# Making the two column halves of attention's P v product neighbours on TensorE in a hybrid attention and mLSTM layer

## The chip, the cores and the metric

The kernel runs on one core of a Trainium2 chip. The metric is the device time in microseconds (us) of one execution. The engines are named as the profile names them: PE is the matmul side of TensorE and PEld its weight loads, DVE is VectorE, ACT is ScalarE, POOL is GpSimd and SP is SyncE, which here only issues DMAs.

## The reference

One layer mixes sliding window attention with an mLSTM (a gated linear recurrence), adds a residual and a layer norm, and runs a SwiGLU feed-forward block with a second layer norm. The model width is 1024. There are 2048 prompt tokens behind 16 meta tokens, and 64 sample tokens. Attention has 8 query heads of 64 features, and two key and value heads, so four query heads share each of them. Cut to what matters here:

```python
s = einsum('nbqkgd,nbskd->nbkgqs', q, k) * HEAD_DIM ** -0.5      # kd = 64, k: the 2 kv heads, g: 4 query heads of each
s = where(mask, s + alibi, -inf)                                 # window of 128
p = exp(s - mx);  p = p / (sum(p) + exp(sink - mx))
att = einsum('nbkgqs,nbskd->nbqkgd', p, v)                       # the P v product
y  = concat([head_norm(att), head_norm(sigmoid(o) * h_m)])       # h_m: the mLSTM
x1 = layer_norm(alpha * x + y @ w_out)
out = layer_norm(alpha * x1 + (silu(x1 @ w_gate) * (x1 @ w_up)) @ w_down)
```

## The kernel before

The work has three phases. Phase 1a and 1b project the input onto q, k, v, the gates and the conv channels; phase 2, over five groups of 384 to 440 tokens, does the output projection, the layer norms and the feed-forward block. All large products are written as three matmuls of split operands, in the helper `mm3` (L123, L124 and L125: upper bits by upper bits, upper by lower, lower by upper). They are the bulk of PE's work. Their weights are fetched by SP (`wtile`, L995), rounded to the upper bits on ACT (L111), and the rest is taken on DVE or POOL (L120).

Attention and the mLSTM are background work. For each of the 16 chunks of 128 prompt tokens there is one generator `bg_attn(c)` and one `bg_ml(c)`; `both` steps them side by side, and `pace` takes steps of the queue between the large products, from the second column group of phase 1b on. `bg_drain` finishes the chunks that the next token group needs. The program written in this order goes through the framework's scheduler, which sets each engine's final order: by operands, buffers and its own estimate of when each operand is ready, an instruction may be moved past others of its engine. On the chip each engine then takes its queue in that order, and a semaphore wait at the head holds what stands behind it.

Within a chunk `bg_attn` works as follows. The scores of the 8 heads go to the SBUF tile `Pt`. For each half `j` of the 256 keys, the four heads of kv head `g` are transposed on PE into a PSUM tile (L542, matmuls with the identity in `C`), and ACT copies that tile to the SBUF tile `p` (L544, one copy for each `g`). Then, for each `g`, one matmul (L548) multiplies the 64 value columns of kv head `g` with `p`:

```python
        for c0, n, j in halves:
            ps = []
            for g in range(2):
                pt = bps()
                for t in range(4):
                    PE.transpose(pt[0:n, 128 * t:128 * t + 128], Pt[:, 4 * g + t, c0:c0 + n], ident)   # L542
                p = t2k("pt", [128, 512], 4)
                A.copy(p[0:n], pt[0:n])                                                                # L544
                ps.append(p)
            yield
            for g in range(2):
                PE.matmul(o[64 * g:64 * g + 64, :], lhsT=vt[0:n, j, 64 * g:64 * g + 64], rhs=ps[g][0:n],   # L548
                          start=(j == 0), stop=(j == 1), skip_group_check=True)
            yield
```

The weights of that matmul are 128 rows by 64 columns, and the result of `g` lies on the PSUM partitions 64 g to 64 g + 63: the two matmuls use different column halves of the array. They are float32, and each appears in the trace as two passes of 512 columns. In all there are 16 chunks, 2 halves of the keys and 2 kv heads: 64 matmuls, 32 pairs. After the second pair ACT reads `o` (L553), and a norm of each head follows (`att_rstd`, L470 to L478).

The other background matmuls that stand beside them are those of the mLSTM (L667, L677 and L678) and the transposes of its output (L592).

Of the kernel before, what the change touches and what calls it, by code (L numbers as in the profile page):

```python
# [20 lines left out]
NS = 64  # L21
# [10 lines left out]

# column offsets of the packed constants and parameters
C_T, C_U, C_BD, C_ID, C_QS, C_US, C_MS, C_SEL, C_SS = 0, 256, 384, 512, 640, 644, 708, 772, 780
# [15 lines left out]
def tile_hymba(  # L50
# [16 lines left out]
    cp = ctx.enter_context(tc.tile_pool(name="const", bufs=1))  # L67
    # the first weights and columns of phase 1b lie where the background work is later
    early = ExitStack()
# [10 lines left out]

# [1 line left out]
    C = cp.tile([128, C_END], F32, name="C")  # L82
# [16 lines left out]

    # token-major gate results: columns (chunk, head), chunk 0 the meta tokens  # L100
    NC4 = (NCH + 1) * 4
# [5 lines left out]

# [1 line left out]
    def hi_of(eng, out, src):  # L109
# [7 lines left out]
    def split(eng, hi, lo, src, veng=V):  # L117
        """src (float32) -> hi, its upper bits, and lo, the rest."""
        hi_of(eng, hi, src)
        return veng.tensor_tensor(out=lo, in0=src, in1=hi.bitcast(F32), op=ALU.subtract)  # L120
# [6 lines left out]
    def rsqrt(v, y, t):  # L127
        """y = v ** -0.5 (v positive, float32): integer seed and Newton's steps."""
        V.tensor_scalar(out=t.bitcast(I32), in0=v.bitcast(I32), scalar1=1, scalar2=None,
                        op0=ALU.logical_shift_right)  # L130
        V.tensor_scalar(out=y.bitcast(I32), in0=t.bitcast(I32), scalar1=-1.0,
                        scalar2=float(0x5F3759DF), op0=ALU.mult, op1=ALU.add)
        for _ in range(3):
            V.tensor_tensor(out=t, in0=v, in1=y, op=ALU.mult)
            V.scalar_tensor_tensor(out=t, in0=t, scalar=-0.5, in1=y, op0=ALU.mult, op1=ALU.mult)
            V.scalar_tensor_tensor(out=y, in0=t, scalar=1.5, in1=y, op0=ALU.add, op1=ALU.mult)

    flip = [0]

    # weights and columns of phase 1b; the order of its tiles: c first, the conv and the maps follow  # L140
    MT = [5, 6, 7, 8, 0, 1, 2, 3, 4]
    NEARLY = 4
    # the last columns' q and k come later, while the first layer norm runs
    NMT = [9, 9, 9, 9, 9 - NLATE]
# [35 lines left out]

# [1 line left out]
    with ExitStack() as s1:  # L182
# [39 lines left out]

        # the first two tiles of tokens go through the weights as they arrive
        x0, x1 = (load_x(tiles[i], ((0, 2), (2, KD)), "v") for i in range(2))
# [4 lines left out]
        for k in range(KD):  # L229
# [8 lines left out]
            for i in range(2):  # L238
                mm_a(start[i], i, k)
        # nothing else is fetched before the weights of this phase  # L240
        with tc.issue_after(w1dma[0].ins):
            constants()
        for i in range(NCH + 1):
# [23 lines left out]
            vm = st[:, 128:128 + 516].rearrange("p (h e) -> p h e", e=129)  # L267
            # v, centred over the head dimension for the attention
            sm = tp.tile([128, 2], F32, tag="sm", name="sm", bufs=2)
# [31 lines left out]

# [1 line left out]
    def gates():  # L303
# [24 lines left out]
        V.tensor_scalar(out=u, in0=e, scalar1=1.0, scalar2=None, op0=ALU.add)  # L328
        # log1p(e) = ln(u) + (e - (u - 1)) / u, u = fl(1 + e)
        V.scalar_tensor_tensor(out=d, in0=u, scalar=-1.0, in1=e, op0=ALU.add, op1=ALU.subtract)  # L330
# [6 lines left out]
        Us = C[0:NS, C_US:C_US + NS]  # L337
        # b: running sums of log f, token-major and as rows (chunk, head)
        b = bps()
# [35 lines left out]
        V.tensor_copy(bl, rb[0:1, 0:NC4])  # L375
        # m of each chunk's end: m = b_last + max(m, max a)
        for h in range(4):
# [14 lines left out]
        A.dma_start(out=GW.rearrange("r g t -> r (g t)"), in_=gw)  # L392
        # back to tokens on partitions
        mb = bps()
# [7 lines left out]
        V.tensor_tensor(out=ENM[:, 0:NC4], in0=gt[:, 0:NC4], in1=bsb[:, 0:NC4], op=ALU.add)  # L402
        # the running sequences: segments of 8 tokens
        cms = tmp(NS, 4)
# [34 lines left out]

# [1 line left out]
    def t2k(tag, shape, bufs, dt=F32):  # L441
        return bp.tile(shape, dt, tag=tag, name=tag, bufs=bufs)

    def spread_rstd(sq, n, nc_, ind, ni, space):
        """sq: tiles [128 features, nc_ * n tokens] to be added; sums over the features with ind [128, ni] give the
        variances with tokens on partitions; then their rsqrt, spread over the features (PSUM)"""
        vp = space()
# [19 lines left out]
    def att_rstd(o, w):  # L467
        """rsqrt of the variances of the heads of o ([128 (kv, d), w], centred), over all of d"""
        sq = t2k("pt", [128, 512], 4)
# [14 lines left out]
    def bg_attn(c):  # L484
# [52 lines left out]
# [3 lines that stand above are left out]
# [3 lines left out]
                p = t2k("pt", [128, 512], 4)  # L543
                A.copy(p[0:n], pt[0:n])  # L544
                ps.append(p)
            yield
            for g in range(2):
                PE.matmul(o[64 * g:64 * g + 64, :], lhsT=vt[0:n, j, 64 * g:64 * g + 64], rhs=ps[g][0:n],  # L548
                          start=(j == 0), stop=(j == 1), skip_group_check=True)
            yield  # L550
# [12 lines left out]
    def mlstm_tail(nd, n, enm, o, y0):  # L563
        """nd: two PSUM tiles [n, 2, 129] of num | den; writes the normed output to y columns y0."""
        dn = t2k("dn", [128, 64], 2)
# [264 lines left out]
    def both(*gens):  # L830
        """steps of all of them, side by side"""
        gens = list(gens)
        while gens:
            for x in list(gens):
                if next(x, 0) == 0:
                    gens.remove(x)
            yield

    # background queue: (column up to which it counts, columns needed, number of steps, generator)
    queue = [(NM, NM, 1, bg_meta())]  # L840
# [19 lines left out]
    def bg_drain(col):  # L860
        """finish everything that columns up to col need"""
        while done[0] < len(queue) and queue[done[0]][0] <= col:
# [16 lines left out]
    def out_q(pool, p, m, c0, w):  # L879
        """feature tile m of q (m < 4) or k of the columns from c0 on"""  # L880
        ev = pool.tile([128, 426], F32, tag="ev", name="ev", bufs=4) if pool is not None else x_tile(F32)
# [9 lines left out]
    def need(g):  # L891
        # chunks are whole: the column where the last one that group g reads ends
        e = ends[g]
# [3 lines left out]

# [1 line left out]
    with ExitStack() as s1:  # L899
# [5 lines left out]
        for g, w in enumerate(IN_GROUPS):  # L905
            c0 = sum(IN_GROUPS[:g])
            wp_ = w if g < 4 else w - NS      # meta and prompt columns of the group

            def conv(h):
                """conv + SiLU of head h over the group's columns -> 2 * c_act"""  # L910
                e, es = ext[g, h]
# [76 lines left out]

# [1 line left out]
    with ExitStack() as s2:  # L990
# [11 lines left out]
        def weights():  # L1002
            """the tiles of the weights in the order of their use"""
            for g in range(len(FF_GROUPS) + 1):
# [71 lines left out]
        def norm(z, w, s, space, fast=False):  # L1076
            """z: tiles, s: the sum of all of them, or of all but the last if fast;
            centres z in place, returns 1 / standard deviation (PSUM)"""
            mu = space()
# [24 lines left out]
        def ln1(z, w, s, out, fast=False, marks={}):  # L1104
            ry = yield from norm(z, w, s, gps, fast)
            for k in range(KD):
# [5 lines left out]
                if k % 2 == 0:  # L1112
                    continue
                # the rest of the even tile on DVE, of the odd one on Pool
                ze, be = z[k - 1][:, 0:w], Q[:, Q_L1B + k - 1:Q_L1B + k]
# [42 lines left out]
        def down(z, h, s, w, zs, adds):  # L1158
            """adds the products of slice s of the hidden features to z"""
            n = SLICES[s]  # L1160
# [25 lines left out]
        x1 = []  # L1186
        # the chain to the first x1 goes ahead of the background work
        mark = {7: None}
# [56 lines left out]

# [1 line left out]
def _consts():  # L1247
# [30 lines left out]
def _layout(x):  # L1278
    """the arrays of setup_inputs() as the kernel reads them"""
    f = {n: np.asarray(a) for n, a in x.items()}  # L1280
    cat = np.concatenate
    X = cat([f["meta_tokens"], f["x_prompt"][0], f["x_sample"].reshape(NS, D)], 0)

    def feat(w):          # (K, N) -> [p, k, N]
        return w.reshape(-1, 128, w.shape[1]).transpose(1, 0, 2)

    def mtile(w):         # (K, M) -> [p, m, k * 128 + j]
        k, m = w.shape
# [76 lines left out]
```

## Time and profile before

| | |
|---|---|
| time, median of 3 runs | 2522.82 us (2521.44 to 2523.54) |
| span of the profiled execution | 2522.3 us |
| PE busy | 2465.8 us (98%) |
| PEld busy | 2267.9 us (90%) |
| DVE busy | 1506.0 us (60%) |
| ACT busy | 954.8 us (38%) |
| POOL busy | 330.5 us (13%) |
| matmul passes on PE | 13135 |
| mean granted TensorE clock | 0.991 |

The profile gives no time for the profiled execution other than its span; the span lies 0.5 us under the median of the runs. PE's busy time counts a matmul from its start to its modelled end, and neighbours overlap. So what a matmul costs is read from the start of one to the start of the next, in the timeline.

### The profile page before, as it was taken

Reading aid. Unit: us, or ns where it says so; the run is one execution under the profiler, and the core shown is the slowest. Engines: PE = TensorE matmul, PEld = TensorE weight load, DVE = VectorE, ACT = ScalarE, POOL = GpSimd, SP = SyncE. Lnnn points to the kernel's source line nnn. Section 1 sums busy time; section 2 is a strip of 40 time slices with the busy share of each in tenths; the row PEclk is TensorE's granted clock in tenths of the full one; section 3 lists DMA queues with packets and bytes.
Section 4 is the critical chain, followed back from the end, with each engine's and each line's share of the span. In section 5 each row is a group of like instructions: output and inputs, shape, how many; then the busy total and the mean of one; then the engine's idle time right before and its main releaser. Section 6 shows DMA issues by size and latency. Waiting matters only on the chain.

```text
span 2522.3 us, 34923 instructions
## 1 busy us (share of the span) xinstructions
PE 2465.8 (98%) x13135; PEld 2267.9 (90%) x13135; DVE 1506.0 (60%) x3129; ACT 954.8 (38%) x1730; POOL 330.5 (13%) x253
## 2 busy tenths in 40 slices
PE   9999999998999999999999999999999999999997
PEld 8999888887999888888989889889999999999997
DVE  6223466547876887656664976666676434664444
ACT  3112444345434444424333543443353223442332
POOL 1000000021000015210011500100330000520001
PEclk9999999999999999999999999999999999999998
DMA  7223533664444543554443354444344333343442
GB/s 234 88 89 89 168 113 123 124 218 118 137 133 136 150 142 94 179 155 142 122 137 115 103 186 123 129 126 123 100 147 134 115 109 113 113 137 115 119 126 77
DMA packets 197330, 327.89 MB, mean 130 GB/s; under 512 B 31010, under 2 KB 133498, under 8 KB 197146
## 3 DMA queue, kind: packets, MB, share of 16 engines
q1 hardware_dynamic: 170400, 294.29, 39.9%
q10 hardware_dynamic: 26762, 31.36, 3.8%
q8 instruction: 104, 1.70, 0.3%
q14 instruction: 64, 0.52, 0.1%
HBM read 281.59 MB, written 44.99 MB: 129 GB/s over the span
## 4 chain that ended last, share of the span: by engine, by line
PE 88%; DVE 4%; DMA 4%; ACT 1%; issue 1%; POOL 0%; SPq 0%; ACTq 0%; DVEq 0%; POOLq 0%
PE gps L123 24%; PE gps L125 24%; PE gps L124 24%; PE bps L548 2%; PE bps L123 2%; PE bps L125 2%; PE bps L124 2%; PE bps L513 2%; DMA w<-in_wo 1%; PE bps L542 1%; PE gps L932 1%; DVE w L120 1%; PE bps L677 1%; PE bps L650 1%; PE bps L667 1%
## 5 line engine op out<-in xcount | busy, mean ns | idle before, releaser
L125 PE MATMUL gps<-x,w 128*128 128x440 f32 (+4 forms) x2240 | 797.3, 356 | 3.9 <-POOL w L120 3.3
L123 PE MATMUL gps<-x,w 128*128 128x440 f32 (+4 forms) x2240 | 790.4, 358 | 7.9 <-DVE z L1070 4.5
L124 PE MATMUL gps<-x,w 128*128 128x440 f32 (+4 forms) x2240 | 795.6, 356 | 0.6 <-DVE x L1117 0.5
L111 ACT CAST w<-w 128x1024 fp32r<-128x1024 f32 (+2 forms) x423 | 400.4, 947 | 783.9 <-DMA w<-in_wd 277.5
L120 DVE TENSOR_TENSOR w<-w 128x1024 fp32r<-128x1024 f32 (+2 forms) x391 | 442.8, 1133 | 361.9 <-ACT w L111 197.9
L123 PEld LDWEIGHTS gps<-x,w 128*128 128x128 f32 x2240 | 421.8, 188 | 32.3 <-DVE z L1070 6.2
L125 PEld LDWEIGHTS gps<-x,w 128*128 128x128 f32 x2240 | 421.6, 188 | 24.6 <-POOL w L120 5.0
L124 PEld LDWEIGHTS gps<-x,w 128*128 128x128 f32 x2240 | 421.2, 188 | 23.8 <-issue 5.2
L123 PE MATMUL gps<-hh,w 128*128 128x440 f32 (+2 forms) x880 | 314.4, 361 | 0.0
L125 PE MATMUL gps<-hh,w 128*128 128x440 f32 (+2 forms) x880 | 312.5, 356 | 0.0
L124 PE MATMUL gps<-hl,w 128*128 128x440 f32 (+2 forms) x880 | 312.0, 356 | 0.0
L120 POOL TENSOR_TENSOR w<-w 128x1024 fp32r<-128x1024 f32 x32 | 77.0, 2407 | 778.0 <-ACT w L111 676.8
L123 PEld LDWEIGHTS gps<-hh,w 128*128 128x128 f32 x880 | 165.6, 188 | 9.9 <-issue 3.5
L125 PEld LDWEIGHTS gps<-hh,w 128*128 128x128 f32 x880 | 165.6, 188 | 8.7 <-issue 1.0
L124 PEld LDWEIGHTS gps<-hl,w 128*128 128x128 f32 x880 | 165.8, 188 | 7.9 <-issue 1.5
L1167 DVE SCALAR_TENSOR_TENSOR z<-z,gps 128x440 f32<-128x440 f32 (+2 forms) x160 | 92.9, 589 | 68.6 <-PE gps L125 67.9
L111 ACT CAST hh<-hr 128x440 fp32r<-128x440 f32 (+2 forms) x110 | 59.9, 545 | 157.2 <-DVE hr L1153 157.0
L1153 DVE SCALAR_TENSOR_TENSOR hr<-ft,gps 128x440 f32<-128x440 f32 (+2 forms) x110 | 64.9, 590 | 83.7 <-PE gps L125 83.3
L120 DVE TENSOR_TENSOR hl<-hr,hh 128x440 fp32r<-128x440 f32 (+2 forms) x110 | 82.3, 748 | 29.1 <-ACT hh L111 28.7
L1150 ACT ACTIVATE ft<-gps 128x440 f32<-128x440 f32 (+2 forms) x110 | 57.3, 521 | 104.1 <-PE gps L125 103.5
L1061 POOL TENSOR_TENSOR zs<-zs,z 128x440 f32<-128x440 f32 (+2 forms) x58 | 81.7, 1408 | 101.7 <-DVE z L1070 66.6
L120 DVE TENSOR_TENSOR x<-x 128x426 fp32r<-128x426 f32 (+4 forms) x80 | 48.0, 612 | 78.3 <-ACT x L111 56.6
(338 smaller groups left out, 3150.0 us busy)
## 6 DMA issues: line engine op xcount, KB each, us to landing
w<-in_wg SPq DMA_DIRECT2D x110, 512.0 KB, 3.7
w<-in_wu SPq DMA_DIRECT2D x110, 512.0 KB, 3.7
w<-in_wd SPq DMA_DIRECT2D x80, 384.0 KB, 3.2
w<-in_wd SPq DMA_DIRECT2D x80, 320.0 KB, 3.0
w<-in_wo SPq DMA_DIRECT2D x40, 512.0 KB, 3.9
FM<-ev ACTq DMA_DIRECT2D x52, 213.0 KB, 2.0
TM<-st ACTq DMA_DIRECT2D x16, 578.0 KB, 3.9
vmo<-TM SPq DMA_DIRECT2D x16, 514.0 KB, 3.5
```

The costliest lines, as they stand in the source:

```text
L111: A.copy(out, src)
L120: return veng.tensor_tensor(out=lo, in0=src, in1=hi.bitcast(F32), op=ALU.subtract)
L123: PE.matmul(out, lhsT=wh, rhs=xh, start=start, stop=False)
L124: PE.matmul(out, lhsT=wh, rhs=xl, start=False, stop=False)
L125: PE.matmul(out, lhsT=wl, rhs=xh, start=False, stop=stop)
L513: PE.matmul(s[g][:, j, 0:nk], lhsT=x[r, 2 * tt + j, :], rhs=y[r, 0:nk], start=(i == 0), stop=(i == 2))
L542: PE.transpose(pt[0:n, 128 * t:128 * t + 128], Pt[:, 4 * g + t, c0:c0 + n], ident)
L548: PE.matmul(o[64 * g:64 * g + 64, :], lhsT=vt[0:n, j, 64 * g:64 * g + 64], rhs=ps[g][0:n], start=(j == 0), stop=(j == 1), skip_group_check ...
L1061: G.tensor_tensor(out=s[:, 0:w], in0=s[:, 0:w], in1=z[m][:, 0:w], op=ALU.add)
L1150: A.activation(out=t[:, 0:w], in_=pgt[:, 0:w], func=AF.Tanh, scale=0.5)
L1153: V.scalar_tensor_tensor(out=hr[:, 0:w], in0=t[:, 0:w], scalar=0.5, in1=pu[:, 0:w], op0=ALU.mult, op1=ALU.mult)
L1167: V.scalar_tensor_tensor(out=zm, in0=zm, scalar=ALPHA if s == 0 else 1.0, in1=p[:, 0:w], op0=ALU.mult, op1=ALU.add)
```

## The change

When `g` is 0, the matmul gets one more dependency: on the copy of `g` = 1, whose result it doesn't read. Nothing is computed otherwise, and no instruction of an engine is added or removed. The other differences of the two files are comments and blank lines. Line numbers from the matmul on are higher in the changed file: L549 is the P v matmul there, and from L550 on 5 is added to the old number (the mLSTM's L667, L677 and L678 are L672, L682 and L683).

```diff
                 p = t2k("pt", [128, 512], 4)
-                A.copy(p[0:n], pt[0:n])
+                cp2 = A.copy(p[0:n], pt[0:n])
                 ps.append(p)
             yield
+
             for g in range(2):
-                PE.matmul(o[64 * g:64 * g + 64, :], lhsT=vt[0:n, j, 64 * g:64 * g + 64], rhs=ps[g][0:n],
-                          start=(j == 0), stop=(j == 1), skip_group_check=True)
+                mm = PE.matmul(o[64 * g:64 * g + 64, :], lhsT=vt[0:n, j, 64 * g:64 * g + 64], rhs=ps[g][0:n],
+                               start=(j == 0), stop=(j == 1), skip_group_check=True)
+                if g == 0:
+                    tc.add_manual_dep(mm.ins, cp2.ins.name,
+                                      mybir.DependencyInfo(mybir.DependencyClass.Sync, mybir.DependencyReason.DATA),
+                                      reason="both halves of P v at once")
             yield
```

At that point `cp2` is the copy of the last `g`, that is of `g` = 1. The scheduler sees the dependency, so the order of PE changes. Of the 32 pairs 11 stand as neighbours on PE before; with the change all 32 do.

The first place is PE's order in chunk 3, first half of the keys, early in the feed-forward block of the first token group (in the trace about 600 us after the start). The names are output and inputs: `pt` and `vt` are the transposed P and v, `S` and `qs`, `vmo` and `gm` are the mLSTM's operands, `x` and `w` those of the large products. Before:

```order
L125 MATMUL gps<-x,w 128x384
L123 MATMUL gps<-x,w 128x384
L548 MATMUL bps<-pt,vt 64x512
L677 MATMUL bps<-S,qs 128x129
L678 MATMUL bps<-vmo,gm 128x129
L548 MATMUL bps<-pt,vt 64x512
L677 MATMUL bps<-S,qs 128x129
L678 MATMUL bps<-vmo,gm 128x129
L542 MATMUL bps<-C,P 128x128 x8
```

With the change, at the same place of PE's order:

```order
L123 MATMUL gps<-x,w 128x384
L124 MATMUL gps<-x,w 128x384
L549 MATMUL bps<-pt,vt 64x512 x2
L682 MATMUL bps<-S,qs 128x129
L683 MATMUL bps<-vmo,gm 128x129
L682 MATMUL bps<-S,qs 128x129
L683 MATMUL bps<-vmo,gm 128x129
L542 MATMUL bps<-C,P 128x128 x8
```

The second half has moved up beside the first, ahead of the mLSTM's matmuls, and the transposes of the other keys' half follow as before.

The second place is PE's order in chunk 4, first half of the keys (about 647 us), where the first half stood right behind the second copy's transposes. Before, with the second half 15 rows further down:

```order
L542 MATMUL bps<-C,P 128x128 x5
L667 MATMUL bps<-wkv,ktm 128x129 x2
L542 MATMUL bps<-C,P 128x128 x3
L548 MATMUL bps<-pt,vt 64x512
L677 MATMUL bps<-S,qs 128x129
L678 MATMUL bps<-vmo,gm 128x129
L677 MATMUL bps<-S,qs 128x129
L678 MATMUL bps<-vmo,gm 128x129
```

With the change, where the pair stands 18 rows behind the last transposes (17 matmuls of the large products lie between):

```order
L123 MATMUL gps<-hh,w 128x384
L124 MATMUL gps<-hl,w 128x384
L549 MATMUL bps<-pt,vt 64x512 x2
L682 MATMUL bps<-S,qs 128x129
L683 MATMUL bps<-vmo,gm 128x129
L682 MATMUL bps<-S,qs 128x129
L683 MATMUL bps<-vmo,gm 128x129
L542 MATMUL bps<-C,P 128x128 x8
```

Here the first half has moved down to the second, and the mLSTM's matmuls behind it have moved down with it; the large products' matmuls have moved up into the place.

## Prediction

> **What bounds the kernel now.** I read the page's busy shares and its chain of waits first, then PE's list of waits, then busy time by stage, and last the timeline around L548.
>
> ```profile
> span 2522.3 us, 34923 instructions
> ...
> PE 2465.8 (98%) x13135; PEld 2267.9 (90%) x13135; DVE 1506.0 (60%) x3129; ACT 954.8 (38%) x1730; POOL 330.5 (13%) x253
> ...
> PE 88%; DVE 4%; DMA 4%; ACT 1%; issue 1%; POOL 0%; SPq 0%; ACTq 0%; DVEq 0%; POOLq 0%
> ```
>
> PE is busy for all but 56.5 us, and 88% of the chain that ended last is PE. A step that PE no longer issues therefore shortens the run, unless something that PE now waits for does not move with it. PE's waits (total, times, longest):
>
> ```profile
> PE gps L462 <- DVE rs L136: 8.1, 5, 3.5
> PE gps L123 <- ACT ev L882: 6.2, 2, 5.4
> ...
> PE gps L932 <- ACT ev L882: 4.5, 1, 4.5
> ...
> PE gps L125 <- POOL w L120: 3.3, 4, 1.6
> ```
>
> No wait of PE's matmuls for an attention operand is long enough to be among them. The waits belong to layer norms and to the passage from phase 1b to phase 2. Two stages (start:end and length, then busy time of each engine):
>
> ```profile
> 500.00:600.00 100.00, 86.54 (x454) 79.11 (x452) 55.72 (x104) 46.10 (x87) 21.43 (x15) 0.91 0.60 173
> 600.00:1100.00 500.00, 494.24 (x2748) 441.84 (x2747) 370.46 (x854) 206.01 (x410) 75.01 (x53) 1.00 0.47 139
> ```
>
> Columns are PE, PEld, DVE, ACT, POOL, clock, DMA share and GB/s. From 600 to 1100 us PE is full and DVE, the next engine, is busy for 370 of 500 us. Between 500 and 600 us PE has 13.5 us of holes.
>
> **What the change removes.** A P v half that stands alone, between matmuls on the full array:
>
> ```profile
> 324.96 0.36 PE L124 MATMUL gps<-x,wbh 128*128 128x426 f32 x1
> 325.16 0.36 PE L125 MATMUL gps<-x,wbl 128*128 128x426 f32 x1
> 325.45 1.07 PE L548 MATMUL bps<-pt,vt 128*64 128x512 f32 x2
> 326.45 0.46 PE L123 MATMUL gps<-x,wbh 128*128 128x426 f32 x1
> 326.75 0.35 PE L124 MATMUL gps<-x,wbh 128*128 128x426 f32 x1
> 326.94 0.36 PE L125 MATMUL gps<-x,wbl 128*128 128x426 f32 x1
> ```
>
> Its two passes hold PE from 325.45 to 326.45, 1.00 us. Two halves that are neighbours already:
>
> ```profile
> 378.06 1.08 PE L548 MATMUL bps<-pt,vt 128*64 128x512 f32 x4
> 379.07 0.46 PE L123 MATMUL gps<-x,wbh 128*128 128x426 f32 x1
> 379.37 0.36 PE L124 MATMUL gps<-x,wbh 128*128 128x426 f32 x1
> ```
>
> Four passes take 1.01 us: the second half runs beside the first. Two lone halves take 2.00 us, so a pair that is brought together saves 0.99 us.
>
> It saves a visit to the half-array shape as well. In the first fence the step from one large matmul to the next is 0.19 to 0.20 us (324.96 to 325.16, 326.75 to 326.94), but 0.29 us ahead of L548 and 0.30 us just behind it: about 0.20 us for a visit. Among the mLSTM's matmuls the price behind a visit is the same:
>
> ```profile
> 601.89 1.07 PE L548 MATMUL bps<-pt,vt 128*64 128x512 f32 x2
> 602.89 0.49 PE L677 MATMUL bps<-S,qs 128*128 128x129 f32 x2
> 603.22 0.39 PE L678 MATMUL bps<-vmo,gm 128*128 128x129 f32 x2
> ...
> 648.33 0.39 PE L677 MATMUL bps<-S,qs 128*128 128x129 f32 x2
> 648.55 0.39 PE L678 MATMUL bps<-vmo,gm 128*128 128x129 f32 x2
> ```
>
> From L677 to L678 it is 0.33 us after L548 and 0.22 us elsewhere. A pair brought together thus saves 0.99 + 0.20 = 1.19 us of PE.
>
> How many pairs are apart now follows from L548's busy time by stage (PE and PEld busy, passes):
>
> ```profile
> 300.00:500.00 200.00, 10.73 (x24) 1.91 (x24) 0.99 0.44 118
> ...
> 600.00:1100.00 500.00, 24.66 (x48) 4.40 (x48) 1.00 0.47 139
> 1100.00:1700.00 600.00, 19.34 (x48) 3.48 (x48) 1.00 0.45 133
> 1700.00:2522.00 822.00, 2.16 (x8) 0.40 (x8) 0.99 0.40 118
> sum 2222.00, PE 56.88 PEld 10.19; mean PE 11.38 PEld 2.04
> ```
>
> A lone half is 1.07 us busy and a pair 1.08 us. 64 halves in 56.88 us are 42 lone ones and 11 pairs (44.9 + 11.9 = 56.8). The order shows the same 11, and 32 with the change. By stage the same division gives 4 split pairs before 500 us, 11 from 600 to 1100 us, 6 from 1100 to 1700 us, none later. Their worth is 4.8, 13.1 and 7.1 us. **The sum is 21 x 1.19 = 25.0 us.** If the visits' price isn't saved, because matmuls are regrouped elsewhere, it is 21 x 0.99 = 20.8 us; I take the upper end, since rows at both kinds of neighbours show the price.
>
> **What the change adds: a wait.** The first half waits for the second copy, and PE's queue behind it waits too. Where the copies and the halves stand, at the second place of the order and at the latest copy that I found (ACT's rows are the copies):
>
> ```profile
> 646.35 0.49 PE L542 MATMUL bps<-C,P 128*128 128x128 f32 x3
> 646.77 1.07 PE L548 MATMUL bps<-pt,vt 128*64 128x512 f32 x2
> ...
> 646.88 0.58 ACT L544 COPY pt<-bps 128x512 f32<-128x512 f32 x1 [0.30 <-PE bps L542]
> ...
> 870.27 0.27 PE L542 MATMUL bps<-C,P 128*128 128x128 f32 x1
> ...
> 872.71 0.58 ACT L544 COPY pt<-bps 128x512 f32<-128x512 f32 x1
> 876.04 1.04 ACT L111 CAST w<-w 128x1024 fp32r<-128x1024 f32 x1 [2.75 <-DMA w<-in_wu]
> ```
>
> At 646.77 the first half ran before the second copy had ended (647.46), and in the old order the new wait would have cost 0.7 us. But the order changes with the dependency. There the pair now stands behind 17 more large matmuls, about 17 x 0.17 to 0.19 = 2.9 to 3.2 us after the transposes, which ended at 646.84; the copy comes 0.6 us after them. That is over 2 us in hand. The copy at 872.71 ended 2.75 us after its transposes, and still inside 3 us. So I cost the wait itself at nothing: the large matmuls of `mm3` that moved ahead of the pair hide it. If ACT is held longer, as it was for the 2.75 us ahead of 876.04 by a weight that had not landed, a pair may wait: from 0 to 2.75 us each time.
>
> Who waits for the pair? ACT's read of `o`, two mLSTM steps (moved down with it at the second place), and the buffers of `p`. SP's queue holds DMAs that wait for chunk results, but in the trace PE's waits list none of them. No DMA is moved by itself.
>
> **What is given back.** Ahead of 500 us PE gains 4.8 us, and there the end is the passage to phase 2, where ACT is late (5.4 and 4.5 us above). The DMAs that crowd in there start late:
>
> ```profile
> 479.23 0.33 SPq L995 DMA_DIRECT2D w<-in_wo  x1
> ```
>
> That fetch waits for a buffer which PE's last group of phase 1b frees, so I expect it to move forward with PE: give-back between 0 and 4.8 us, taken near 0. In phase 2 PE asks for weights up to 2.6% earlier (13.1 of 500 us). PE waits four times for POOL's part of a weight, 3.3 us in all; I allow one more of the longest, 1.6 us, and 0.4 us for late copies. Give-back 2.0 us; below nothing is possible too, since the moved background work may also shorten a wait such as the 5.4 us.
>
> So 2522.8 - 25.0 + 2.0 = 2499.8 us. The profiled span would be 2522.3 - 23.0 = 2499.3 us; it stood 0.5 us under the median, and I keep that distance.
>
> [...] The rows of weight loads for the pair and for a lone half:
>
> ```profile
> 378.06 0.20 PEld L548 LDWEIGHTS bps<-pt,vt 128*64 128x64 f32 x4 [0.61 <-issue]
> ...
> 325.44 0.19 PEld L548 LDWEIGHTS bps<-pt,vt 128*64 128x64 f32 x2 [0.29 <-issue]
> ```
>
> The second half's loads add 0.01 us, so they go beside the first half's work. [...]
>
> **Rivals.**
> - *The halves don't overlap once they are neighbours*: the second half's weights wait until the first half's matmul has left the array, or the parts of a pair still start apart. The gain is 21 x 0.20 = 4.2 us: 2518.6 us, no change. Against it stands the pair at 378.06. Chance 3%.
> - *Slower: the new wait holds PE.* ACT serves weights, activations and copies in order; if it is late, PE stands at the head of the pair. The point from which it decides: 25.0 us over 32 pairs, a mean stall of 0.78 us. With 1.5 us each: 2522.8 - 25.0 + 48.0 = 2545.8 us. For it speaks the one copy that came 2.75 us after its transposes; against it, the 3 us that the new order leaves. Chance 3%.
> - *Other streams take part of it back.* The 4.8 us are lost at the passage to phase 2, and half of the 13.1 us from 600 to 1100 us to weights that come no sooner: 2522.8 - 25.0 + 4.8 + 6.5 = 2509.1 us. For it: 13.5 us of holes between 500 and 600 us, DVE at 74% in the next stage. Against: PE's waits for weights are 3.3 us in all. Chance 15%.
> - *The moved background work shortens a wait* by about the 5.4 us above: 2492 us. Chance 8%.
>
> **How the numbers follow.** The forecast, 2495 to 2505 us, has 70%, and 1% is for anything else. The range 2493 to 2510 us takes in the lower sum (2522.8 - 20.8 + 2 = 2504), most of the give-back and part of the shortened waits, some 85%. 0.2%, 5.0 us, is about what a measurement of this kernel can tell from no change: faster means under 2517.8 us. Faster 0.93 (forecast, give-back, shortened waits), same 0.04, slower 0.03.
>
> **What would show it.** L548, then L549, busy for 32 x 1.08 = 34.6 us in place of 56.88, every timeline row of it with four passes and about 1.01 us to the next start; PE's busy time down by 24 to 25 us and its idle time near 56.5 us; no PE wait for ACT's `pt`. The forecast is wrong if such a wait appears among PE's longest, or if the waits at 490 to 580 us grow by what the stage before gained.

## The result, and the profile after

| | before | after |
|---|---|---|
| time, median of 4 runs | 2522.13 us (2519.01 to 2523.54) | 2506.24 us (2504.97 to 2508.94) |
| span of the profiled execution | 2522.3 us | 2507.1 us |
| PE busy, and the rest of the span | 2465.8, 56.5 us | 2444.7, 62.4 us |
| mean granted TensorE clock | 0.991 | 0.989 |

The ratio of the times is 0.9938 (0.9925 to 0.9952): the change makes the kernel faster by 15.9 us between the medians. The forecast was 2499.8 us, 23.0 us under the median of before that it started from (2522.82 us): the time came out 6.4 us above it, and the gain 7.1 us short. The profiled execution of after took 2508.94 us, 1.8 us more than its span.

The page of after, and its chain of waits by engine:

```profile
span 2507.1 us, 34929 instructions
...
PE 2444.7 (98%) x13135; PEld 2267.2 (90%) x13135; DVE 1514.9 (60%) x3129; ACT 955.3 (38%) x1730; POOL 328.3 (13%) x253
...
PE 88%; DVE 4%; DMA 4%; ACT 1%; issue 1%; POOL 0%; SPq 0%; ACTq 0%; DVEq 0%; POOLq 0%
```

The bound is the same as before: PE carries 88% of the chain. Its busy time fell by 21.1 us, and the time in which it stood idle grew by 5.9 us.

The P v product of after by stage (columns as before: stage, length, PE and PEld busy with passes, clock, DMA share, GB/s), and its pair at the second place of the order:

```profile
600.00:1100.00 500.00, 11.87 (x44) 2.17 (x44) 0.99 0.47 142
1100.00:1700.00 600.00, 12.94 (x48) 2.37 (x48) 1.00 0.43 133
...
sum 2207.10, PE 34.51 PEld 6.32; mean PE 6.90 PEld 1.26
```

```profile
646.51 0.34 PE L124 MATMUL gps<-hl,w 128*128 128x384 f32 x1
646.77 1.08 PE L549 MATMUL bps<-pt,vt 128*64 128x512 f32 x4
647.78 0.49 PE L682 MATMUL bps<-S,qs 128*128 128x129 f32 x2
```

All 32 pairs are neighbours: 34.51 us for 128 passes, 1.08 us for four, where before it was 56.88. From the pair to the next matmul it is 1.01 us. So the intended gain is there, in full. What PE waits for now (total, times, longest):

```profile
PE gps L462 <- DVE rs L136: 9.8, 4, 3.4
PE gps L123 <- ACT ev L887: 6.8, 1, 6.8
...
PE gps L125 <- POOL w L120: 2.7, 3, 1.4
...
PE bps L743 <- DVE P L741: 2.2, 1, 2.2
```

No wait is for ACT's copies at L544. L462, the spreading of a layer norm's result, waited 8.1 us in all and waits 9.8. L743, a transpose in the attention of the sample tokens, was not among the waits of before at all.

To see where the gain is lost I compared the start of the same (n-th) matmul of the large products, L123 to L125, in the two traces; there are 11184 of them in each. The lead of after, worked out from the two starts, swings by a few microseconds where background work stands on different sides of a place, and at quieter places it is:

| time in after, us | 468 | 590 | 734 | 760 | 1048 | 1700 | 1804 | 1828 | end |
|---|---|---|---|---|---|---|---|---|---|
| lead over before, us | 5.6 | 4.7 | 9.3 | 4.3 | 9.3 | 17.6 | 17.8 | 14.0 | 15.1 |

The lead grows by what the pairs are worth, and drops twice: by 5.0 us between 734 and 760 us and by 3.8 us between 1804 and 1828 us. The timeline of after at the first drop (POOL, DVE and PE; one undisturbed L741 stands below):

```profile
736.29 2.88 POOL L120 TENSOR_TENSOR w<-w 128x1024 fp32r<-128x1024 f32 x1 [26.03 <-DVE pt L134]
...
736.89 2.40 DVE L741 TENSOR_SCALAR P<-P,mx 128x192 f32<-128x192 f32 x1
...
739.44 0.30 PE L743 MATMUL bps<-C,P 128*128 128x128 f32 x1 [2.19 <-DVE P L741]
...
744.47 0.52 PE L123 MATMUL gps<-x,w 128*128 128x384 f32 x1
744.78 0.52 PE L124 MATMUL gps<-x,w 128*128 128x384 f32 x1
...
751.57 0.32 DVE L741 TENSOR_SCALAR P<-P,mx 128x192 f32<-128x192 f32 x1
```

POOL splits a weight tile here (of the tiles of 1024 columns it gets those whose number is a multiple of eight, 32 in all). While it runs, a DVE instruction that takes 0.32 us elsewhere takes 2.40 us, and it ends 0.12 us behind POOL. PE's queue stands 2.19 us for its result. Then the large matmuls follow each other at 0.31 us in place of 0.17 us. The stretches around it, all engines (PE, PEld, DVE, ACT, POOL, then the clock, DMA share, GB/s):

```profile
737.00:741.00 4.00, 1.30 (x9) 0.64 (x8) 3.96 (x4) 1.11 (x3) 2.18 (x1) 0.98 0.09 29
741.00:748.00 7.00, 7.00 (x24) 5.78 (x24) 4.55 (x12) 2.03 (x5) 0.00 (x0) 0.53 0.72 225
748.00:760.00 12.00, 12.00 (x71) 11.97 (x71) 6.79 (x13) 4.75 (x8) 0.00 (x0) 1.00 0.44 138
```

PE is busy for all of 741 to 748 us, but its granted clock is 0.53: a half-speed stretch of 6.8 us by the clock's record, which by an estimate from that clock costs half of it, 3.4 us, and counts as busy time. The second drop, in after:

```profile
1805.68 0.36 PE L125 MATMUL gps<-hh,w 128*128 128x440 f32 x1
...
1806.20 2.34 POOL L120 TENSOR_TENSOR w<-w 128x1024 fp32r<-128x1024 f32 x1 [1.61 <-ACT w L111]
...
1806.23 2.33 DVE L136 SCALAR_TENSOR_TENSOR rs<-rs 110x4 f32<-110x4 f32 x1
...
1808.61 1.54 PE L462 MATMUL gps<-C,rs 110*128 110x110 f32 x8 [2.57 <-DVE rs L136]
...
1809.83 0.71 PE L123 MATMUL gps<-hh,w 128*128 128x440 f32 x1
```

and the same place in before:

```profile
1823.45 0.36 PE L125 MATMUL gps<-hh,w 128*128 128x440 f32 x1
...
1823.99 0.16 DVE L136 SCALAR_TENSOR_TENSOR rs<-rs 110x4 f32<-110x4 f32 x1
...
1824.21 1.14 PE L462 MATMUL gps<-C,rs 110*128 110x110 f32 x8 [0.40 <-DVE rs L136]
...
1824.45 2.39 POOL L120 TENSOR_TENSOR w<-w 128x1024 fp32r<-128x1024 f32 x1 [2.09 <-ACT w L111]
...
1825.12 0.45 PE L123 MATMUL gps<-hh,w 128*128 128x440 f32 x1
```

In before POOL's instruction starts 0.3 us after the last step of the layer norm's chain of small DVE instructions; in after it starts 0.03 us ahead of it, and the 0.16 us step takes 2.33 us. The lead over these rows is 17.77 us at L125 and 15.29 us at the next L123; a half-speed stretch of 3.4 us behind the hole (granted clock 0.50 from 1809.2 to 1812.6 us) takes the rest. Before has one such collision too, in another norm:

```profile
983.72 2.34 POOL L120 TENSOR_TENSOR w<-w 128x1024 fp32r<-128x1024 f32 x1 [1.23 <-ACT w L111]
...
983.75 2.33 DVE L136 SCALAR_TENSOR_TENSOR rs<-rs 110x4 f32<-110x4 f32 x1
```

and after keeps it: there L136 of the same norm takes 2.29 us at 975.70 us, and L462 waits 3.41 us, for 3.55 us in before.

How many such meetings there are can be counted. DVE instructions that take over 1.5 us longer than the median of their line and form number 7 in before, all beside L120 on POOL, and 13 in after, 12 of them beside L120. Of those 13, only the three at 737, 976 and 1806 us have a hole of over 2 us on PE right behind them.

The two spans differ by 15.2 us, and this can be split into three parts. PE is busy for 22.3 us within the half-speed stretches of the clock's record in before and for 32.1 us in after. With half of that taken as lost (an estimate), PE's work at full speed falls from 2454.7 to 2428.7 us, by 26.0 us. The half-speed stretches take back 4.9 us and the idle time 5.9 us. So the theory to test was: the pairs bring their 25 us, and the new order puts two more of DVE's short, urgent instructions beside POOL's split, which costs about 9 us with the half-speed stretches behind the holes. The rival: the loss is spread over the run (weights and other streams that come no sooner), and the holes stand at places where some wait would end late anyway.

### The profile page after: what moved, and what is told of

Its sections match the earlier page's. It is cut to its first block, busy times and chain, and to the rows that moved or that the text cites. A ratio compares the mean times of both kernels' runs of the same rounds, so it can differ in the third digit from the quotient of the medians.

```text
span 2507.1 us, 34929 instructions
## 1 busy us (share of the span) xinstructions
PE 2444.7 (98%) x13135; PEld 2267.2 (90%) x13135; DVE 1514.9 (60%) x3129; ACT 955.3 (38%) x1730; POOL 328.3 (13%) x253
## 4 chain that ended last, share of the span: by engine, by line
PE 88%; DVE 4%; DMA 4%; ACT 1%; issue 1%; POOL 0%; SPq 0%; ACTq 0%; DVEq 0%; POOLq 0%
PE gps L123 25%; PE gps L125 24%; PE gps L124 24%; PE bps L123 2%; PE bps L125 2%; PE bps L124 2%; DMA w<-in_wo 1%; PE bps L513 1%; PE bps L549 1%; PE bps L542 1%; PE gps L937 1%; DVE w L120 1%; PE bps L682 1%; PE bps L655 1%; PE bps L672 1%
## 5 line engine op out<-in xcount | busy, mean ns | idle before, releaser
L123 PE MATMUL gps<-x,w 128*128 128x440 f32 (+4 forms) x2240 | 792.3, 358 | 11.1 <-DVE z L1075 5.6
L125 PE MATMUL gps<-x,w 128*128 128x440 f32 (+4 forms) x2240 | 797.9, 357 | 3.4 <-POOL w L120 2.7
L124 PE MATMUL gps<-x,w 128*128 128x440 f32 (+4 forms) x2240 | 794.0, 356 | 0.6 <-DVE x L1122 0.6
L120 DVE TENSOR_TENSOR w<-w 128x1024 fp32r<-128x1024 f32 (+2 forms) x391 | 441.5, 1130 | 359.7 <-ACT w L111 185.4
L123 PEld LDWEIGHTS gps<-x,w 128*128 128x128 f32 x2240 | 422.4, 189 | 36.5 <-DVE z L1075 7.4
L125 PEld LDWEIGHTS gps<-x,w 128*128 128x128 f32 x2240 | 422.6, 189 | 23.3 <-POOL w L120 4.4
L124 PEld LDWEIGHTS gps<-x,w 128*128 128x128 f32 x2240 | 422.6, 189 | 18.4 <-DVE x L1122 0.9
L123 PE MATMUL gps<-hh,w 128*128 128x440 f32 (+2 forms) x880 | 314.8, 362 | 1.4 <-DVE z L1172 1.3
L125 PE MATMUL gps<-hh,w 128*128 128x440 f32 (+2 forms) x880 | 313.1, 357 | 0.0
L124 PE MATMUL gps<-hl,w 128*128 128x440 f32 (+2 forms) x880 | 312.5, 356 | 0.0
L123 PEld LDWEIGHTS gps<-hh,w 128*128 128x128 f32 x880 | 166.1, 189 | 11.9 <-issue 4.6
L124 PEld LDWEIGHTS gps<-hl,w 128*128 128x128 f32 x880 | 166.3, 189 | 8.1 <-issue 1.5
L125 PEld LDWEIGHTS gps<-hh,w 128*128 128x128 f32 x880 | 166.1, 189 | 7.4 <-issue 0.5
L120 POOL TENSOR_TENSOR w<-w 128x1024 fp32r<-128x1024 f32 x32 | 77.4, 2419 | 727.1 <-ACT w L111 475.2
L120 DVE TENSOR_TENSOR hl<-hr,hh 128x440 fp32r<-128x440 f32 (+2 forms) x110 | 83.8, 762 | 27.6 <-ACT hh L111 27.3
L1066 POOL TENSOR_TENSOR zs<-zs,z 128x440 f32<-128x440 f32 (+2 forms) x58 | 80.0, 1379 | 102.0 <-DVE z L1075 66.3
L1156 DVE SCALAR_TENSOR_TENSOR ft<-ft,gps 128x440 f32<-128x440 f32 (+2 forms) x110 | 64.7, 588 | 46.4 <-ACT ft L1155 46.3
```

Of the source, the lines that this page charges most:

```text
L123: PE.matmul(out, lhsT=wh, rhs=xh, start=start, stop=False)
L124: PE.matmul(out, lhsT=wh, rhs=xl, start=False, stop=False)
L125: PE.matmul(out, lhsT=wl, rhs=xh, start=False, stop=stop)
L1066: G.tensor_tensor(out=s[:, 0:w], in0=s[:, 0:w], in1=z[m][:, 0:w], op=ALU.add)
L1156: V.scalar_tensor_tensor(out=t[:, 0:w], in0=t[:, 0:w], scalar=1.0, in1=pgt[:, 0:w], op0=ALU.add, op1=ALU.mult)
```

## The experiments

Each was timed beside runs of before on its own chip; those medians lie between 2525.91 and 2528.22 us, so ratios are compared, and a time saved is one minus the ratio times that median.

**Is the loss set by the order?** After once more, with nothing edited.

> The changed kernel once more, with a new profile. In its first profile 25 us of PE's work are gone, but 10 us are given back: 6 us more idle time of PE and 3 us more in stretches in which the clock was granted at half speed. Theory (collisions set by the order): the idle time at 737 and 1806 us, each with a half-speed stretch behind it, stands again at the same places within 1 us, since it follows from the order of POOL's and DVE's work; time 2504 to 2509 us, 15 to 18 us under the kernel before. Rival (chance of one execution): the holes lie elsewhere or are gone, and the times of its executions spread by more than 5 us.

Measured: 2511.16 us, 0.9942 (0.993 to 0.9955), 14.7 us saved, a little less than the 15 to 18 us expected. Its executions spread over 7.4 us (2509.0 to 2516.38 us), which the rival had named as its sign, so the places of the holes decide. The same two waits, in the list of waits of this execution:

```profile
PE gps L462 <- DVE rs L136: 9.9, 4, 3.5
...
PE bps L743 <- DVE P L741: 2.2, 1, 2.2
```

and the second of the two holes in its timeline:

```profile
1811.63 1.14 PE L462 MATMUL gps<-C,rs 110*128 110x110 f32 x8 [2.54 <-DVE rs L136]
...
1812.83 0.36 PE L124 MATMUL gps<-hl,w 128*128 128x440 f32 x1
1813.03 0.36 PE L125 MATMUL gps<-hh,w 128*128 128x440 f32 x1
```

The holes are there again, within 0.03 us, so they belong to the order. The half-speed stretch is not: behind this hole the large matmuls run at full speed at once (0.20 us from L124 to the next).

**Which stage loses it?** The dependency in part of the chunks. The split pairs of these parts are those of the three stages: worth 4.8, 13.1 and 7.1 us by the prediction.

```diff
-                if g == 0:
+                if g == 0 and c <= 2:          # dep_c0_2
+                if g == 0 and 3 <= c <= 8:     # dep_c3_8
+                if g == 0 and c >= 9:          # dep_c9_15
```

> The dependency in chunks 0 to 2 alone: 4 split pairs become neighbours (15 of 32 in all). Work taken from PE: 4 x 1.19 = 4.8 us. Theory (gain by pair, loss at a few places): 4 to 6 us faster than before, since the first profile of the changed kernel was 5.6 us ahead at 470 us. Rival (the passage to phase 2 swallows what is gained before it): under 2 us. Rival (40% of every gain is given back): 2.9 us.

> The dependency in chunks 3 to 8 alone: 11 split pairs become neighbours (22 of 32). Work taken from PE: 13.1 us. Theory (gain by pair, loss at a few places, most of them in this stage): 4 to 8 us faster if the hole at 737 us stands here too, 11 to 13 us if it doesn't. Rival (40% of every gain is given back): 7.9 us with no such hole.

> The dependency in chunks 9 to 15 alone: 6 split pairs become neighbours (17 of 32). Work taken from PE: 7.1 us. Theory (gain by pair, loss at a few places): 6 to 7 us faster, or 3 to 4 us if a hole in the layer norm near 1820 us opens as it did in the changed kernel. Rival (40% of every gain is given back): 4.3 us with no such hole.

Measured: 0.9985 (0.9976 to 0.9994), 0.998 (0.9971 to 0.999) and 0.9973 (0.9964 to 0.9982): 3.8 us (1.5 to 6.1), 5.0 us (2.5 to 7.3) and 6.8 us (4.5 to 9.1) saved of 4.8, 13.1 and 7.1. They add up to 15.6 us, about what the whole change saves on this chip. By the medians the first and the last part keep nearly all they are worth, and the second loses 8 us, though the interval of the first is too wide to tell it from its rivals. The timeline of the second part:

```profile
742.38 2.58 POOL L120 TENSOR_TENSOR w<-w 128x1024 fp32r<-128x1024 f32 x1 [29.25 <-ACT w L111]
...
742.66 2.42 DVE L741 TENSOR_SCALAR P<-P,mx 128x192 f32<-128x192 f32 x1
```

The collision is there, with a hole of 1.89 us, one of 0.51 us and a half-speed stretch of 6.8 us: 5.8 us. The first part has neither of the two collisions. The last part's profile has one of its own (L135 of the same norm takes 2.24 us at 1821.76 us, and L462 waits 2.55 us); with such a hole the theory had said 3 to 4 us, which the median misses, though the interval leaves room for the 2.55 us alone, since no half-speed stretch follows this hole. The parts thus tell the stage of the main loss, not yet its cause.

**Is it POOL's split?** First only the tiles that collide: two weight tiles of POOL's go to DVE.

```diff
-            split(..., G if n == 8 and (wcount[0] % WP == 0 or ...) else V)
+            split(..., G if n == 8 and (wcount[0] % WP == 0 and wcount[0] not in (48, 264) or ...) else V)
```

> The changed kernel, with the lower part of two weight tiles (number 48 and 264, those at 736 and 1806 us) taken on DVE in place of POOL. Theory (POOL's 2.4 us operation holds one DVE operation, and at these two places that one is in a short chain that PE waits for): the holes of 2.7 us at 737 and 2.5 us at 1806 and the half-speed stretch of 6.8 us behind the first go, 8 to 10 us in all; time 23 to 26 us (0.9 to 1.0%) under the kernel before. Rival (PE is ahead of its suppliers and waits somewhere in any case): holes of the same size elsewhere, time within 3 us of the changed kernel, 15 us under before.

Measured: 2506.97 us, 0.9918 (0.9906 to 0.9931), 20.7 us saved, 6 us more than after by the ratios (their intervals touch) and less than the 23 to 26 us that the theory said. Both holes are gone: L741 takes 0.32 us again, and L462 waits 0.51 us at 1807 us, as short as in before (0.40 us). The order has changed at the first place as well, where L743 now comes 3.2 us behind L741. But a third hole grew:

```profile
973.62 2.34 POOL L120 TENSOR_TENSOR w<-w 128x1024 fp32r<-128x1024 f32 x1 [0.34 <-ACT w L111]
...
973.73 2.24 DVE L135 SCALAR_TENSOR_TENSOR rs<-rs 110x4 f32<-110x4 f32 x1
```

L462 of the norm at 976 us now waits 5.9 us, 3.4 us in after, and a half-speed stretch of 6.8 us begins within the hole, at 974.7 us. POOL holds the norm's chain no longer here than in after (2.24 us for 2.29), so the 2.5 us by which the hole grew are not from the split. Moving two tiles has changed the order elsewhere too. So a wider test takes all of POOL's splits away, with the change and without it; POOL keeps its other 221 instructions.

```diff
-            split(..., G if n == 8 and (wcount[0] % WP == 0 or ...) else V)
+            split(..., V)
```

> The kernel before, with the lower part of every weight tile on DVE, none on POOL (DVE gets 32 x 1.2 = 38 us more of work). It serves as the base of the next run. Theory (collisions): the 3.6 us hole at 984 us shrinks by about 2 us, since its chain is held by POOL's operation there; time 0 to 6 us under before. Rival (DVE becomes late with weights): 3 us or more over before.

> The changed kernel, with the lower part of every weight tile on DVE, none on POOL. Theory (the give-back comes from collisions with POOL's operations): against the same kernel without the change (the run beside it) 20 to 25 us faster, close to the 25 us of PE's work. Rival (other streams take back a share of any gain): 13 to 17 us faster than that kernel, as with POOL.

Measured: before with no split on POOL 2528.88 us, 1.0009 (1.0 to 1.0018); after with none 2504.24 us, 0.9912 (0.9898 to 0.9925). Without POOL's splits the change saves 24.6 us, and not the 15 us that it saves beside them; with the intervals of both ratios that is about 20 to 29 us. Without the splits no DVE instruction of before, and one of after (beside L783 on POOL), takes over 1.5 us longer than the median of its form, and in after PE's idle time (56.3 us) and its busy time at half speed (21.3 us) are back at the level of before with them.

That 24.6 us lies so near to the prediction's 25.0 us is in part luck. Before itself does not gain, where I had expected 0 to 6 us: its hole stayed at 3.41 us. DVE's own split of the tile stands there now, in the midst of the norm's chain, and the next step, 0.16 us elsewhere, ends with another POOL instruction (L1061, 1.92 us from 987.01). The timeline of before without POOL's splits:

```profile
986.86 1.22 DVE L120 TENSOR_TENSOR w<-w 128x1024 fp32r<-128x1024 f32 x1
...
987.99 0.95 DVE L136 SCALAR_TENSOR_TENSOR rs<-rs 110x4 f32<-110x4 f32 x1
```

After without the splits has no hole at this norm. In its order the chain isn't interrupted, and L462 does not wait. Of the 27.7 us between the spans of these two kernels 5.5 us are half-speed time (PE is busy at half speed for 32.3 us in the one and 21.3 us in the other, taken half), and PE's work at full speed falls by 22.4 us.

The waits and the page of after with no split on POOL:

```profile
PE gps L462 <- DVE rs L136: 4.8, 3, 3.8
...
PE gps L125 <- DVE w L120: 4.0, 6, 1.4
```

```profile
PE 2443.3 (98%) x13135; PEld 2263.4 (91%) x13135; DVE 1514.7 (61%) x3161; ACT 954.8 (38%) x1730; POOL 253.8 (10%) x221
```

L743's wait is gone, and L462's is half of what it was. The work moved to DVE costs little there: PE waits 4.0 us for DVE's weights, where it waited 2.7 us for POOL's.

**One more tile.** Tile 96, the one of the hole at 974 us, is taken from POOL too.

```diff
-            ... wcount[0] not in (48, 264) ...
+            ... wcount[0] not in (48, 96, 264) ...
```

> As the run with two tiles moved, and with weight tile 96 on DVE as well: its POOL operation at 973.6 us held the layer norm's chain there for 2.2 us and opened a hole of 6.0 us. Theory (collisions set by the order): that hole shrinks to 1 to 2 us and the half-speed stretch of 6.8 us behind it goes; 4 to 7 us under the run with two tiles, 1.0 to 1.1% under the kernel before. Rival: the next collision takes its place, within 2 us of that run, 0.8%.

Measured: 2507.81 us, 0.9919 (0.9904 to 0.9934): nothing over the two tiles, the theory's 4 to 7 us are missed. The hole is still 5.80 us, and the timeline shows DVE's queue in place of POOL's split:

```profile
967.79 0.95 DVE L120 TENSOR_TENSOR w<-w 128x768 fp32r<-128x768 f32 x1
...
968.66 0.98 DVE L136 SCALAR_TENSOR_TENSOR dn<-dn 128x4 f32<-128x4 f32 x1
...
971.76 0.95 DVE L120 TENSOR_TENSOR w<-w 128x768 fp32r<-128x768 f32 x1
...
972.63 0.15 DVE L455 TENSOR_SCALAR rs<-gps 110x4 f32<-110x4 f32 x1
...
975.75 1.22 DVE L120 TENSOR_TENSOR w<-w 128x1024 fp32r<-128x1024 f32 x1
...
976.89 0.96 DVE L136 SCALAR_TENSOR_TENSOR rs<-rs 110x4 f32<-110x4 f32 x1
```

The norm's chain starts at 972.63 us (L455), though the matmuls that it reads ended before 969: two weight tiles and the mLSTM's norm stand ahead of it on DVE. Its last step stands behind a third weight tile and, at 0.96 us, beside another instruction of POOL (L1066, 1.84 us from 975.98), with whose end its own falls within 0.03 us. That this order causes the hole is read from the timeline, and was not tried.

**What is the overlap itself worth?** Both halves write the same partitions, 0 to 63, and are added there; partitions 64 to 127 are set to zero. Of the 32 pairs 31 stay neighbours.

```diff
+        V.memset(o[64:128, :], 0.0)
...
-                mm = PE.matmul(o[64 * g:64 * g + 64, :], ..., start=(j == 0), stop=(j == 1), ...)
+                mm = PE.matmul(o[0:64, :], ..., start=(j == 0 and g == 0), stop=(j == 1 and g == 1), ...)
```

> The changed kernel, but both products of a pair write PSUM partitions 0 to 63, the same column half of the array (the second kv head is added to the first and the other half is filled with zeros by DVE, so the attention result is another one). 31 of 32 pairs are still neighbours. Theory (the gain is the overlap of the two column halves, 0.99 us a pair, and the visits saved are worth 4 us): no pair overlaps, 32 x 0.99 = 32 us over the changed kernel, 15 to 18 us over the kernel before; a pair takes 1.9 to 2.0 us to the next matmul. Rival (being neighbours is what counts, by fewer changes of the array's shape and a better order): within 5 us of the changed kernel.

Measured: 2530.62 us, 1.0013 (1.0004 to 1.0021), 3.3 us slower than before, where the theory had said 15 to 18 us. A pair in its timeline:

```profile
375.13 1.93 PE L550 MATMUL bps<-pt,vt 128*64 128x512 f32 x4
376.99 0.47 PE L123 MATMUL gps<-x,wbh 128*128 128x426 f32 x1
```

It is 1.86 us to the next matmul, 1.01 us in after. The overlap is worth 0.85 us a pair, and standing together without overlap 0.14 us (2.00 us for two lone halves). Over after, the 31 pairs should cost 31 x 0.85 = 26.4 us; the theory had taken 0.99 us for each of 32. By the ratios it is 0.0071, some 18 us. The other 8 us are again the order: this one has no hole longer than 0.6 us at either collision. The three parts of the spans say the same: PE's work at full speed is 27.0 us more than in after, its idle time 6.2 us less, and its half-speed time costs 2.5 us less. The weight loads tell the same of the pair: PEld is busy for 14.78 us with them here, and for 6.32 us in after.

**A version faster than before and after.** The order of before leaves the score products (L513), 64 rows each, one kv head after the other in places. A chain of order-only dependencies makes the heads alternate, with no split on POOL.

```diff
+            m1 = None
...
-                        PE.matmul(s[g][:, j, 0:nk], lhsT=x[r, 2 * tt + j, :], rhs=y[r, 0:nk], ...)
+                        ms = PE.matmul(s[g][:, j, 0:nk], lhsT=x[r, 2 * tt + j, :], rhs=y[r, 0:nk], ...)
+                        if m1 is not None:
+                            tc.add_manual_dep(ms.ins, m1.ins.name,
+                                              mybir.DependencyInfo(mybir.DependencyClass.NoSync,
+                                                                   mybir.DependencyReason.SCHED_ONLY), ...)
+                        m1 = ms
```

> The changed kernel without POOL's weight work, and with each chunk's 12 score products (L513, 64 rows by 128 columns, the two kv heads on the two row halves of the array) kept in turn by a chain of dependencies on PE, so that the row halves run side by side more often. Theory (neighbours overlap, also for row halves): 6 products of one kv head alone take 0.90 us and 12 of both 0.91; eight groups are split so in the changed kernel, and the chain leaves one product of a group alone at 0.3 us: 8 x 0.6 = 5 us less of PE; 3 to 6 us under the kernel without POOL's weight work alone, 1.0 to 1.1% under before. Rival (the chain holds the scores back and the chunk's later steps come late): no gain or a loss.

Measured: 2500.54 us, 0.9893 (0.9876 to 0.9909), 27.1 us saved: the fastest median of all. By the ratios it is about 5 us under after with no split on POOL, but the intervals overlap, and the spans differ by 2.5 us (2497.1 for 2499.6), so this last step is not shown clear of noise. The score products in the groups of both (line, form, count, busy, mean ns): ahead of the chain

```profile
L513 PE MATMUL bps<-kt,qt 64*128 64x256 f32 (+1 forms) x384 | 41.8, 299 | 0.0
```

and with it

```profile
L514 PE MATMUL bps<-kt,qt 64*128 64x256 f32 (+1 forms) x384 | 38.0, 302 | 0.0
```

They take 3.8 us less, although the hole at 967 us came back in this order (L462's longest wait is 5.1 us).

## Why the prediction was right in its sum and short in its give-back

The time of 2506.24 us lies in the stated range, 2493 to 2510 us, but outside the 2495 to 2505 us that had 70%.

- *21 split pairs by 1.19 us.* Right. P v is busy for 34.51 us (34.6 said), each pair holds PE for 1.01 us, and PE's work at full speed falls by 26.0 us (25.2 us in the repeat) for the 25.0 us of the sum. The 24.6 us without POOL's splits agree with it in part by luck, as said above. The rival without overlap falls: in all 32 pairs the weight loads of the second half go beside the first (PEld is busy with them for 6.32 us, 0.20 us for the four loads of a pair), and a pair takes 1.01 us, where one that does run one half after the other takes 1.86 us.
- *The new wait costs nothing.* Right. No wait for the copies at L544 is among PE's (one of 0.5 us for a `pt` is L750's, of the sample tokens), and at 646.77 us the second copy, ended at 644.54, was 2.2 us in hand ("over 2 us" said). The slower rival falls with it.
- *The first stage keeps its 4.8 us at the passage to phase 2.* Right in the main: the lead is 5.6 us at 468 us and 4.7 us at 590 us, and the part of chunks 0 to 2 alone saves 3.8 us (1.5 to 6.1). In the traced execution of that part the lead falls from 5.5 to 3.1 us there, so some of it can be lost.
- *Give-back 2.0 us.* This is the term that was mis-sized: 25.0 less 15.2 us of the spans is 9.8 us. The two collisions took 5.0 + 3.8 = 8.8 us of the lead. Away from them it came short of the sum by 2.4 us up to 1700 us (17.6 + 5.0 against 25.0), about the 2.0 us that were allowed for late weights and copies, though PE's waits for POOL's weights fell from 3.3 to 2.7 us and the one late weight, 2.0 us at 523 us for a cast of ACT's, is not in the repeat; and the last stage gave 1.1 us back (14.0 to 15.1). That is 10.1 us. The step that failed is the reading of POOL: the prediction took POOL's split as something that PE waits for when it is late, and not as something that holds DVE while it runs. Before showed it, in the L136 of 2.33 us at 983.75, which the prediction did not use.
- *"PE busy down by 24 to 25 us and its idle time near 56.5 us".* Both off, by that cause: 21.1 us and 62.4 us. The waits for held DVE instructions were idle time (PE busy for 1.30 us of the 4 from 737 us), and the half-speed stretches behind them busy time (all 7.00 us from 741 us). P v's own 22.37 us of it came.
- *Rival: other streams take part back (2509.1 us).* Its time came nearer than the forecast's, but by luck, since its reasons were not seen: of the lead only 0.9 us was lost at the passage, and from 600 us on PE's waits for weights did not grow. *Rival: a shortened wait (2492 us).* Not seen: the waits at 490 us went from 5.4 and 4.5 us to one of 6.8 us (4.9 and 4.1 us in the repeat), but the lead did not grow there.

Why the hole at 970 to 980 us is there in most of these kernels and not in after without splits is read from DVE's order alone, and is open. So is the share of the loss that POOL's split has apart from the order: each run that takes splits away changes the order too.

## What to carry to other kernels

When a dependency reorders the busiest engine, price what it removes from the rows, as here, and then look at which short DVE instructions, with PE waiting behind them, will fall beside a long POOL instruction (of 2.3 to 2.9 us here): the new order drew these meetings anew, 7 beside L120 in before and 12 in after. List, in the trace of before, DVE instructions that take far longer than others of their form; here all 7 of those over 1.5 us longer stood beside a POOL instruction, and the price of such a meeting, where a hole on PE followed (2.2 to 3.6 us in the two traces), was that hole plus the half-speed stretch of 3.4 or 6.8 us behind it. Test the theory with the source of the meetings taken away on both sides of the change, and compare holes and half-speed stretches of the two traces too: every such edit changes the order, and may open or close a hole elsewhere, as moving two tiles did here.

## What the hardware showed that was not expected

- A POOL instruction with 1024 columns (2.34 to 2.88 us) held one DVE instruction until its own end: 0.16 us became 2.33 us, 0.32 us became 2.40 us, and DVE ended 0.02 and 0.12 us behind POOL. DVE's row shows such an instruction as busy (2.33 and 2.40 us), not as waiting.
- A hole of 2.2 us, with one of 0.5 us just behind it, was followed by a half-speed stretch of 6.8 us (granted clock 0.53 from 741 to 748 us) and one of 2.6 us by a stretch of 3.4 us (0.50 from 1809.2 to 1812.6 us); the same hole at 1806 us was followed by one of 3.4 us in one execution and by none in another.
- Two float32 matmuls of 128 rows by 64 columns, each with 512 columns moving through, take 1.01 us as neighbours on different column halves, 1.86 us on the same half, and 2.00 us apart.
